# RWKV-7 chunk inverses on 64x64 tensor-engine tiles in place of 32x32 tiles, with other planner paces

## The chip, the core and the metric

The kernel runs on one core of one Trainium2 chip. The metric is device microseconds (us) of one execution. Engines are named as in the profile: PE (TensorE, matmul), PEld (its weight loads), DVE (VectorE), ACT (ScalarE), POOL (GpSimd), SP (SyncE, which only issues DMAs here).

## The reference

One layer of a hybrid decoder on 512 tokens of width 2048, float32: an input projection, then side by side an RG-LRU branch (4 heads of 256) and an RWKV-7 branch (16 heads of 64), an output projection, a gated FFN of width 6144 with a causal convolution, a gated per-layer embedding, and a final RMSNorm. The part that the change touches is the RWKV-7 scan. Cut to what matters:

```
def step(state, inp):                       # state: per head 64 x 64
    r_t, w_t, k_t, v_t, kk_t, b_t = inp     # b_t = kk_t * a_t
    sa = einsum('bhvk,bhk->bhv', state, -kk_t)
    state = state * w_t + outer(sa, b_t) + outer(v_t, k_t)
    y = einsum('bhvk,bhk->bhv', state, r_t)
```

A chunked form computes this for 64 tokens at once: within a chunk the terms `sa` depend on each other through a strictly triangular 64x64 matrix, so each chunk of each head needs the inverse of a unit triangular 64x64 matrix. There are 8 chunks and 16 heads, so 128 such inverses.

## The kernel before, in words

**Stages.** Phase 1 (about the first 870 us of the profile) holds the input projection, both branches and the half of the output projection that can be done so far. Phase 2 holds the rest of the output projection, the FFN and the gated embedding. Nearly all of the work is dense fp32 matmul done as three fp32r products (high x high, high x low, low x high; lines 156, 158, 160 in phase 1, and 1178 to 1180, 1260 to 1262, 1347 to 1349 in phase 2). Weights come by DMA on SP's queue (L114), ACT makes the high part (L121), DVE the low part (L127) or, for half of phase 1's tiles, POOL by an accumulating DMA (L125).

**The RWKV pairs.** Heads are handled in eight pairs j = 0 to 7; a pair fills the 128 partitions (head 0 in partitions 0 to 63, head 1 in 64 to 127). For each pair there are four generators. `prep(j)` makes the decays and the scaled operands. `batch(j)` makes, for all 8 chunks at once, the score matrices MQ and NQ (L732, L734), the inverse, and two products with it (L741). `chain(j)` carries the 64x64 state through the 8 chunks (L854 to L880). `norm(j)` normalises and gates the output (L889 to L904). `duo(j)` runs `chain(j-1)` and `batch(j)` in lockstep: in each step the chain's products are issued first and the batch's behind them.

**The inverse.** It is built by doubling. With blocks of b = 1, inverses of 2x2 blocks are written down directly from a mask (L765 to L768). For b = 2, 4, 8, 16 a level joins two b-blocks into one of 2b: a first group of products (L775, reads MQ and Tm), a masked copy into Gm by DVE (L785), a second group of products (L775, reads Tt and Gm), an addition into Tm by DVE (L803), and a transpose of Tm into Tt by DVE (L804). Before the change this runs on the four 32x32 diagonal blocks that a pair of heads has (two heads times two halves), so Tm and Tt are 128 x 256 and each group is 8 chunks x 4 blocks = 32 products with a 32-column stationary operand and 16 moving columns. In the trace each fp32 product is two MATMUL instructions, so a group shows as 64. The last join (32 to 64) is done apart: 16 products (L812), two ACT copies into Gm (L815), four ACT copies of Tt into the result TT (L817), 16 products (L825), and two ACT copies of the joined quarter into TT (L827). TT, 128 x 8 x 64, is cleared once at the start by POOL (L291). L741 then multiplies with TT.

**What sets the order.** PE's instruction order in phase 1 is written by a planner, `merge` (L352 to L416). It keeps a virtual time t in ns. A dense matmul costs 216. A step of a core generator (`duo`) yields a cost and a wait; its next step comes when t has passed the larger of that wait and a pace (L375: `dpace` = 3159 while pairs 1 to 7 run in lockstep, `pace` otherwise). `prep` and the two halves of `norm` ("tails") have waits of their own (`start`, `dec7`, `g2`, `g3`). In between, dense matmuls are issued. A dense matmul may also be held until a pair has been prepared or a pair's output is done: the last eight units of the output projection of phase 1 wait for the output of pair 6. The order on the other engines comes from a scheduler that goes by priority; `offw` is the priority of the weight pipeline (L100), `offs` of the core steps, `offd` of what follows dense matmuls, `offp` of prep's steps, `offt` of the transposed operands that `turn` makes (L747 to L753, four of them for each pair).

Of the kernel before, what the change touches and what calls it, by code (L numbers as in the profile page):

```python
# [6 lines left out]
AF = mybir.ActivationFunctionType  # L7
ALU = mybir.AluOpType
# [5 lines left out]
KT = D // 128  # L14
NB = 8

W = dict(offw=3000, offp=[0, 300, 0, 1000, 5000, -100, 466], offl=0, offt=0, pace=1007, dpace=3159, late=8560, offs=10000, offd=3000, start=1554, lora=5885, dec=0, rsk=12832, ready=23343, bonus=39298, t0=5900, tg=1601, tt=1464, lx=4233, lu=1319, ls=1435, g1=97321, g2=4936, g3=7972, per=[2, 3, 2, 2, 2, 2, 3, 0], dec7=6140)
DL = 1024
NP = 8
FF = 6144  # L20
# [2 lines left out]
C = 64  # L23
NC = S // C
# [12 lines left out]
for _n, _c in PCOLS:  # L37
# [1 line left out]
    _o += _c  # L39
PW = _o  # L40

CCOLS = [("ident", 128), ("ones1", 1), ("mask", 128)] + [("lev1", 32)] + [("lev%d" % b, 16) for b in (2, 4, 8, 16)] + \
        [("bd2", 2), ("id32", 32), ("odd", 2)]
CKEEP = 129
COFF = {}
_o = 0
# [6 lines left out]
def shape_constants():  # L53
    c = np.zeros((128, CW), np.float32)
    p = np.arange(128)
    s = p % 64
    t = np.arange(64)
    c[:, COFF["ident"]:COFF["ident"] + 128] = np.eye(128)
    o = COFF["mask"]
    c[:, o:o + 64] = s[:, None] < t[None, :]  # L60
    c[:, o + 64:o + 128] = s[:, None] <= t[None, :]

    r = (p % 32)[:, None]
    t = np.arange(32)[None, :]
    c[:, COFF["lev1"]:COFF["lev1"] + 32] = (t // 2 == r // 2) & (t % 2 == 1) & (r % 2 == 0)

    c[:, COFF["odd"]:COFF["odd"] + 2] = p[:, None] // 32 % 2 == np.arange(2)[None, :]

    for b in (2, 4, 8, 16):
        o = COFF["lev%d" % b]  # L70
        c[:, o:o + 16] = ((r // b) % 2 == 1) & (r // (2 * b) == t[:, :16] // b)
    o = COFF["id32"]
    c[:, o:o + 32] = r == t
    o = COFF["bd2"]
    c[:, o:o + 2] = p[:, None] // 64 == np.arange(2)[None, :]
    c[:, COFF["ones1"]] = 1.0
    return c


class Builder:  # L80
# [160 lines left out]
    def phase1(self):  # L241
# [3 lines left out]
        V, SC, G, TE = nc.vector, nc.scalar, nc.gpsimd, nc.tensor  # L245
# [42 lines left out]
        G.memset(self.scadd[:, :, 0:1], 1.0)  # L288

        self.TT = cp.tile([128, NC, C], F32, name="TT")  # L290
        G.memset(self.TT, 0.0)  # L291

        self.llo = cp.tile([128, 3, 128], F32R, name="llo")
        G.memset(self.llo.bitcast(F32), 0.0)
# [418 lines left out]
    def batch(self, j, q):  # L713
        nc, A, k1 = self.nc, self.A, self.k1
        V, SC, G, TE = nc.vector, nc.scalar, nc.gpsimd, nc.tensor
        T = lambda tag, bufs=1, shape=(128, S), dt=F32: self.t(k1, tag, shape, dt, bufs)
        wk = self.aux
        AR, bt, ktl, vt, pcs, bv, gt = q
        H2 = (slice(0, 64), slice(64, 128))
# [17 lines left out]
        def each(lhs, rhs, dst):  # L737
            ps = wk()
            for c in range(NC):
                for hs in H2:  # L740
                    TE.matmul(ps[hs, c * C:(c + 1) * C], lhs(hs, c), rhs(hs, c), start=True, stop=True)  # L741
            SC.activation(dst, c3(ps), AF.Copy)
# [14 lines left out]
            scores(bt, MQ, half)  # L757

        Q4 = [(slice(32 * g, 32 * g + 32), slice(32 * (g % 2), 32 * (g % 2) + 32)) for g in range(4)]
        Tm, Tt = T("Tm", 1, (128, 8, 32)), T("Tt", 1, (128, 8, 32))
        bc = lambda n, w: self.K(n).unsqueeze(1).broadcast_to([128, 8, w])
        for i, t_ in enumerate((Tm, Tt)):
            V.scalar_tensor_tensor(t_, MQ[:, :, 32 * i:32 * i + 32], self.K("odd")[:, i:i + 1], bc("lev1", 32), ALU.mult, ALU.mult)  # L765
        V.tensor_tensor(Tm, Tm, bc("id32", 32), ALU.add)
        V.tensor_tensor(Tt, Tt, Tm, ALU.add)
        V.transpose(fl(Tm), fl(Tt))  # L768
        yield 2160, W['t0']

        def prod(lhs, rhs):
            ps = wk()
            for i in range(8):
                for r_, c_ in Q4:
                    TE.matmul(ps[r_, i * 16:(i + 1) * 16], lhs(r_, c_, i), rhs(r_, i), start=True, stop=True)  # L775
            return ps[:, 0:128]
        TT = self.TT
        vk = ak = bk = kk2 = None
        for b in (2, 4, 8, 16):

            left = fl(Tm).rearrange("p (g h b) -> p g h b", h=2, b=b)[:, :, 0, :]
            ng = 16 // b
            ps = prod(lambda r_, c_, i: MQ[r_, i, c_], lambda r_, i: left[r_, i * ng:(i + 1) * ng, :])
            Gm = T("Gm", 1, (128, 8, 32))
            V.tensor_tensor(Gm[:, :, 0:16], ps.rearrange("p (i t) -> p i t", t=16), bc("lev%d" % b, 16), ALU.mult)  # L785
            if b == 2:
                scores(ktl, NQ, 0)
            with self.tc.high_priority(offset=W['offt'] - self.OFFS):
                if b == 2:

                    vk = turn("vk", vt, 2)
                    mv = T("mv", 1, (128, NC))
                    V.tensor_reduce(mv.unsqueeze(2), vk, mybir.AxisListType.X, ALU.add)
                    V.scalar_tensor_tensor(vk, mv.unsqueeze(2).broadcast_to([128, NC, C]), -1.0 / C, vk, ALU.mult, ALU.add)
                if b == 4:
                    ak = turn("ak", fl(AR[:, 0]), 1)
                if b == 8:
                    bk = turn("bk", bt, 2)
                if b == 16:
                    kk2 = turn("kk2", ktl, 2)  # L800
            yield 1100, W['tg']
            ps = prod(lambda r_, c_, i: Tt[r_, i, :], lambda r_, i: Gm[r_, i, 0:16])
            V.tensor_tensor(left, ps.rearrange("p (g b) -> p g b", b=b), left, ALU.add)  # L803
            V.transpose(fl(Tt), fl(Tm))  # L804
            if b == 2:
                scores(ktl, NQ, 1)
            yield 1100, W['tt']

        ps = wk()
        for i in range(8):  # L810
            for h in (0, 64):
                TE.matmul(ps[h + 32:h + 64, i * 32:(i + 1) * 32], MQ[h:h + 32, i, 32:64], Tm[h:h + 32, i, :], start=True, stop=True)  # L812
        Gm = T("Gm", 1, (128, 8, 32))
        for h in (32, 96):
            SC.activation(Gm[h:h + 32], ps[h:h + 32, 0:256].rearrange("p (i t) -> p i t", t=32), AF.Copy)  # L815
        for r_, c_ in Q4:
            SC.activation(TT[r_, :, c_], Tt[r_], AF.Copy)  # L817

        X1 = NQ[:, :, 0:64]
        each(lambda hs, c: NQ[hs, c, 0:64], lambda hs, c: vk[hs, c, :], X1)  # L820
        yield 1800, W['tg']
        ps = wk()
        for i in range(8):
            for h in (0, 64):
                TE.matmul(ps[h:h + 32, i * 32:(i + 1) * 32], Gm[h + 32:h + 64, i, :], Tt[h + 32:h + 64, i, :], start=True, stop=True)  # L825
        for h in (0, 64):
            SC.activation(TT[h:h + 32, :, 32:64], ps[h:h + 32, 0:256].rearrange("p (i t) -> p i t", t=32), AF.Copy)  # L827
        yield 860, W['tt']

        WT = MQ[:, :, 0:64]  # L830
        each(lambda hs, c: ak[hs, c, :], lambda hs, c: TT[hs, c, :], WT)
# [5 lines left out]
    def chain(self, j, q, u):  # L837
# [9 lines left out]
        for c in range(NC):  # L847
            yo = py[:, c * C:(c + 1) * C]
            us = NQ[:, c, 0:64]
            last = c == NC - 1  # L850
            if c:
                pu = ch()
                for hs in H2:
                    TE.matmul(pu[hs, 0:64], MQ[hs, c, 0:64], st[hs], start=True, stop=True)  # L854
                us = T("us", 2, (128, 64))
                V.tensor_tensor(us, pu[:, 0:64], NQ[:, c, 0:64], ALU.add)
            if not last:
                ps = ch()
                for hs in H2:
                    TE.matmul(ps[hs, 0:64], kk2[hs, c, :], vk[hs, c, :], start=True, stop=False)  # L860
            for hs in H2:
                TE.matmul(yo[hs], vk[hs, c, :], NQ[hs, c, 64:128], start=True, stop=False)
            if c:
                for hs in H2:
                    TE.matmul(yo[hs], st[hs], AR[hs, 1, c, :], start=False, stop=False)
                yield 700, W['lu']
            if not last:
                for hs in H2:
                    TE.matmul(ps[hs, 0:64], bk[hs, c, :], us[hs], start=False, stop=True)
                pc = pcs[:, c:c + 1]  # L870
                sn = T("st", 2, (128, 64))
                if c == 0:
                    V.tensor_scalar(sn, ps[:, 0:64], pc, None, ALU.mult)
                else:
                    so = T("so", 2, (128, 64))
                    SC.activation(so, st, AF.Copy, scale=pc)
                    V.scalar_tensor_tensor(sn, ps[:, 0:64], pc, so, ALU.mult, ALU.add)
                st = sn
            for hs in H2:
                TE.matmul(yo[hs], us[hs], MQ[hs, c, 64:128], start=False, stop=True)  # L880
            yield 500, W['ls']
# [628 lines left out]
```

## Time and profile before

| what | value |
|---|---|
| median of 3 runs | 2689.41 us (2687.48 to 2691.31) |
| the profiled execution's own time | 2688.0 us |
| its span, first to last instruction | 2686.2 us |
| mean granted TensorE clock | 0.992 |
| PE busy | 2636.5 us, 98% of the span |
| DVE, ACT, POOL busy | 1684.7, 1096.7, 328.5 us |

The span is the profiled execution's time less 1.8 us that lie around it. PE is busy nearly everywhere, so the time is read from PE: from what its instructions take, from where it waits, and from the clock that it is granted. A row of the timeline is: start in us from the span's start, length in us, engine, line and operation, output tile and input tiles, shape of the stationary operand and of the moving one, and the number of instructions merged in the row. Lengths overlap, since matmuls are pipelined; what a group costs PE is the distance from its start to the start of the next row.

### The profile page before, as it was taken

How to read it: one execution, taken by the hardware profiler on the slowest of the kernel's cores; microseconds unless marked ns; L12 is line 12 of the kernel's file. 1: busy time of each engine (PE TensorE's matmuls, PEld its weight loads, DVE VectorE, ACT ScalarE, POOL GpSimd, SP SyncE). 2: the span in 40 equal slices, each digit the busy share in tenths (PEclk: the TensorE clock that was granted, in tenths of full speed). 3: DMA queues.
4: the chain of work that ended last, by engine and by line, in shares of the span. 5: the costliest groups of instructions: out<-in, count | busy, mean ns of one | idle time of the engine just before them, and what ended most of it. 6: DMA issues, size and time to landing. Idle time of an engine off the chain costs nothing.

```text
span 2686.2 us, 43499 instructions
## 1 busy us (share of the span) xinstructions
PE 2636.5 (98%) x18440; PEld 2170.1 (81%) x18440; DVE 1684.7 (63%) x2268; ACT 1096.7 (41%) x1532; POOL 328.5 (12%) x266
## 2 busy tenths in 40 slices
PE   8999999999999999999999999999999999999996
PEld 7887787877777888888888888888888888888886
DVE  6664865667554734667666766766666667775235
ACT  6563555547433533333333333333333333334344
POOL 4120211211131310000000000000000000000013
PEclk9999999999999999999999999999999999999998
DMA  6544443444462422322322223222232222232222
GB/s 191 144 101 102 107 110 92 109 114 105 131 171 67 146 86 88 109 101 96 110 102 94 103 94 110 94 102 102 96 108 102 102 102 102 95 113 87 94 88 101
DMA packets 89235, 286.99 MB, mean 107 GB/s; under 512 B 10320, under 2 KB 13008, under 8 KB 89040
## 3 DMA queue, kind: packets, MB, share of 16 engines
q1 hardware_dynamic: 81984, 258.52, 28.4%
q0 software_dynamic: 7056, 25.69, 5.7%
q8 instruction: 144, 2.36, 0.4%
q14 instruction: 51, 0.42, 0.0%
HBM read 276.05 MB, written 8.13 MB: 106 GB/s over the span
## 4 chain that ended last, share of the span: by engine, by line
PE 91%; DVE 4%; DMA 2%; ACT 1%; POOL 1%; issue 1%; SPq 0%; DVEq 0%; POOLq 0%; ACTq 0%
PE wk L1178 12%; PE wk L1180 12%; PE wk L1179 12%; PE mm L160 7%; PE mm L158 7%; PE mm L156 7%; PE mm L1262 6%; PE mm L1260 6%; PE mm L1261 6%; PE mm L1348 2%; PE mm L1349 2%; PE mm L1347 2%; PE wk L775 2%; PE mm L1178 1%; PE mm L1180 1%; PE mm L1179 1%
## 5 line engine op out<-in xcount | busy, mean ns | idle before, releaser
L121 ACT ACTIVATE whi<-wraw 128x1024 fp32r<-128x1024 f32 (+2 forms) x363 | 375.4, 1034 | 738.5 <-PE mm L158 193.1
L1178 PE MATMUL wk<-uh,whi 128*128 128x512 f32 x1408 | 547.8, 389 | 0.0
L1179 PE MATMUL wk<-ul,whi 128*128 128x512 f32 x1408 | 547.7, 389 | 0.0
L1180 PE MATMUL wk<-uh,wlo 128*128 128x512 f32 x1408 | 547.7, 389 | 0.0
L127 DVE TENSOR_TENSOR wlo<-wraw,whi 128x1024 fp32r<-128x1024 f32 (+2 forms) x314 | 380.6, 1212 | 213.4 <-ACT whi L121 208.5
L121 ACT ACTIVATE whi<-hw 128x1024 fp32r<-128x1024 f32 x154 | 163.2, 1060 | 464.3 <-PE wk L1179 418.6
L160 PE MATMUL mm<-xh,wlo 128*128 128x512 f32 x832 | 333.5, 401 | 7.1 <-DMA wlo<-wz 7.1
L156 PE MATMUL mm<-xh,whi 128*128 128x512 f32 x832 | 331.2, 398 | 1.6 <-DVE y L895 1.6
L158 PE MATMUL mm<-xl,whi 128*128 128x512 f32 x832 | 330.5, 397 | 0.0
L1180 PEld LDWEIGHTS wk<-uh,wlo 128*128 128x128 f32 x1408 | 264.3, 188 | 54.9
L1179 PEld LDWEIGHTS wk<-ul,whi 128*128 128x128 f32 x1408 | 264.3, 188 | 54.8
L1178 PEld LDWEIGHTS wk<-uh,whi 128*128 128x128 f32 x1408 | 264.3, 188 | 54.8
L127 DVE TENSOR_TENSOR wlo<-hw,whi 128x1024 fp32r<-128x1024 f32 x154 | 188.6, 1225 | 181.2 <-ACT whi L121 178.8
L1261 PE MATMUL mm<-wlo,hid 128*128 128x512 f32 x680 | 265.1, 390 | 0.0
L1262 PE MATMUL mm<-whi,hid 128*128 128x512 f32 x680 | 264.8, 389 | 0.0
L1260 PE MATMUL mm<-whi,hid 128*128 128x512 f32 x680 | 264.8, 389 | 0.0
L1206 POOL TENSOR_TENSOR tmp<-tmp,rsa 128x512 f32<-128x512 f32 x48 | 87.4, 1822 | 1360.9 <-ACT tmp L1205 1360.9
L160 PEld LDWEIGHTS mm<-xh,wlo 128*128 128x128 f32 x832 | 156.9, 189 | 42.2 <-DMA wlo<-wz 8.0
L156 PEld LDWEIGHTS mm<-xh,whi 128*128 128x128 f32 x832 | 157.1, 189 | 35.8 <-issue 4.5
L158 PEld LDWEIGHTS mm<-xl,whi 128*128 128x128 f32 x832 | 157.0, 189 | 34.1 <-issue 2.0
L1275 DVE TENSOR_TENSOR h<-h,mm 128x512 f32<-128x512 f32 x264 | 174.8, 680 | 0.7
L1261 PEld LDWEIGHTS mm<-wlo,hid 128*128 128x128 f32 x680 | 127.6, 188 | 26.4
(475 smaller groups left out, 3744.0 us busy)
## 6 DMA issues: line engine op xcount, KB each, us to landing
wraw<-wgu SPq DMA_DIRECT2D x192, 512.0 KB, 3.2
hw<-wd SPq DMA_DIRECT2D x88, 512.0 KB, 3.2
wraw<-wz SPq DMA_DIRECT2D x80, 512.0 KB, 3.6
wlo<-wz POOLq DMA_DIRECT2D x40, 512.0 KB, 5.6
wraw<-wpg SPq DMA_DIRECT2D x31, 512.0 KB, 3.2
wraw<-wo SPq DMA_DIRECT2D x22, 512.0 KB, 3.3
wraw<-wo SPq DMA_DIRECT2D x20, 256.0 KB, 2.9
tmp<-xT SPq DMA_DIRECT2D x16, 256.0 KB, 2.8
```

The source lines that it names most:

```text
L121: nc.scalar.activation(hi, raw, AF.Copy)
L127: nc.vector.tensor_tensor(lo, raw, hi.bitcast(F32), ALU.subtract)
L156: nc.tensor.matmul(ps, hi[:, k, :], xh, start=first and i == 0, stop=False)
L158: nc.tensor.matmul(ps, hi[:, k, :], xl, start=False, stop=False)
L160: nc.tensor.matmul(ps, lo[:, k, :], xh, start=False, stop=last and i == n - 1)
L1178: TE.matmul(ps, wh[:, k, :], xh, start=h + k == 0, stop=False)
L1179: TE.matmul(ps, wh[:, k, :], xl, start=False, stop=False)
L1180: TE.matmul(ps, wl[:, k, :], xh, start=False, stop=h == 1 and k == 7)
L1260: TE.matmul(ps, x[0][:, k, ts_], w[0][:, k, :], start=first and k == 0, stop=False)
L1261: TE.matmul(ps, x[0][:, k, ts_], w[1][:, k, :], start=False, stop=False)
L1262: TE.matmul(ps, x[1][:, k, ts_], w[0][:, k, :], start=False, stop=last and k == 1)
L1275: V.tensor_tensor(o, o, ps[tt], op)
```

## The change

The level loop runs on whole 64x64 chunk matrices: Tm and TT are 128 x 8 x 64 and block diagonal, and the loop has a fifth level, b = 32, in place of the last join done apart. Each group of products is 8 chunks x 2 heads = 16 products with a 64-column stationary operand (MQ or TT) and 32 moving columns. Gm becomes 128 x 256, the transpose of each level 128 x 512. The fifth level's Gm is made by one ACT copy with a 0/1 scale per partition, and its result, the joined quarter, is transposed straight from PSUM into TT by two DVE transposes. The ACT copies at L815, L817 and L827 and POOL's clearing of TT go. Constants are wider (64 and 32 columns in place of 32 and 16). The chain's tiles `us` and `so` have one buffer in place of two. Planner costs and paces change in one line: weight pipeline priority 3000 to 20000, `offd` 3000 to 1000, `offt` 0 to 1000, second entry of `offp` 300 to -100, `pace` 1007 to 1625, `start` 1554 to 1071, `t0` 5900 to 6100, `tg` 1601 to 1750, `tt` 1464 to 2431, `lu` 1319 to 1861, `ls` 1435 to 1231, `g3` 7972 to 13054, `dec7` 6140 to 5046; `dpace`, `late` and the rest stay, and `lx` and `g1` are read nowhere in the code.

```diff
--- before.py
+++ after.py
@@ -14,7 +14,7 @@
 KT = D // 128
 NB = 8
 
-W = dict(offw=3000, offp=[0, 300, 0, 1000, 5000, -100, 466], offl=0, offt=0, pace=1007, dpace=3159, late=8560, offs=10000, offd=3000, start=1554, lora=5885, dec=0, rsk=12832, ready=23343, bonus=39298, t0=5900, tg=1601, tt=1464, lx=4233, lu=1319, ls=1435, g1=97321, g2=4936, g3=7972, per=[2, 3, 2, 2, 2, 2, 3, 0], dec7=6140)
+W = dict(offw=20000, offp=[0, -100, 0, 1000, 5000, -100, 466], offl=0, offt=1000, pace=1625, dpace=3159, late=8560, offs=10000, offd=1000, start=1071, lora=5885, dec=0, rsk=12832, ready=23343, bonus=39298, t0=6100, tg=1750, tt=2431, lx=25915, lu=1861, ls=1231, g1=259468, g2=4936, g3=13054, per=[2, 3, 2, 2, 2, 2, 3, 0], dec7=5046)
 DL = 1024
 NP = 8
 FF = 6144
@@ -39,8 +39,8 @@
     _o += _c
 PW = _o
 
-CCOLS = [("ident", 128), ("ones1", 1), ("mask", 128)] + [("lev1", 32)] + [("lev%d" % b, 16) for b in (2, 4, 8, 16)] + \
-        [("bd2", 2), ("id32", 32), ("odd", 2)]
+CCOLS = [("ident", 128), ("ones1", 1), ("mask", 128)] + [("lev1", 64)] + [("lev%d" % b, 32) for b in (2, 4, 8, 16)] + \
+        [("bd2", 2), ("id64", 64), ("half", 1)]
 CKEEP = 129
 COFF = {}
 _o = 0
@@ -60,17 +60,17 @@
     c[:, o:o + 64] = s[:, None] < t[None, :]
     c[:, o + 64:o + 128] = s[:, None] <= t[None, :]
 
-    r = (p % 32)[:, None]
-    t = np.arange(32)[None, :]
-    c[:, COFF["lev1"]:COFF["lev1"] + 32] = (t // 2 == r // 2) & (t % 2 == 1) & (r % 2 == 0)
-
-    c[:, COFF["odd"]:COFF["odd"] + 2] = p[:, None] // 32 % 2 == np.arange(2)[None, :]
+    r = s[:, None]
+    t = t[None, :]
+    o = COFF["lev1"]
+    c[:, o:o + 64] = (t // 2 == r // 2) & (t % 2 == 1) & (r % 2 == 0)
 
     for b in (2, 4, 8, 16):
         o = COFF["lev%d" % b]
-        c[:, o:o + 16] = ((r // b) % 2 == 1) & (r // (2 * b) == t[:, :16] // b)
-    o = COFF["id32"]
-    c[:, o:o + 32] = r == t
+        c[:, o:o + 32] = ((r // b) % 2 == 1) & (r // (2 * b) == t[:, :32] // b)
+    c[:, COFF["half"]] = s >= 32
+    o = COFF["id64"]
+    c[:, o:o + 64] = r == t
     o = COFF["bd2"]
     c[:, o:o + 2] = p[:, None] // 64 == np.arange(2)[None, :]
     c[:, COFF["ones1"]] = 1.0
@@ -288,7 +288,6 @@
         G.memset(self.scadd[:, :, 0:1], 1.0)
 
         self.TT = cp.tile([128, NC, C], F32, name="TT")
-        G.memset(self.TT, 0.0)
 
         self.llo = cp.tile([128, 3, 128], F32R, name="llo")
         G.memset(self.llo.bitcast(F32), 0.0)
@@ -757,32 +756,30 @@
             scores(bt, MQ, half)
 
 
-
-        Q4 = [(slice(32 * g, 32 * g + 32), slice(32 * (g % 2), 32 * (g % 2) + 32)) for g in range(4)]
-        Tm, Tt = T("Tm", 1, (128, 8, 32)), T("Tt", 1, (128, 8, 32))
-        bc = lambda n, w: self.K(n).unsqueeze(1).broadcast_to([128, 8, w])
-        for i, t_ in enumerate((Tm, Tt)):
-            V.scalar_tensor_tensor(t_, MQ[:, :, 32 * i:32 * i + 32], self.K("odd")[:, i:i + 1], bc("lev1", 32), ALU.mult, ALU.mult)
-        V.tensor_tensor(Tm, Tm, bc("id32", 32), ALU.add)
-        V.tensor_tensor(Tt, Tt, Tm, ALU.add)
-        V.transpose(fl(Tm), fl(Tt))
-        yield 2160, W['t0']
+        Tm, TT = T("Tm", 1, (128, NC, C)), self.TT
+        bc = lambda n, w: self.K(n).unsqueeze(1).broadcast_to([128, NC, w])
+        V.tensor_tensor(TT, MQ[:, :, 0:64], bc("lev1", 64), ALU.mult)
+        V.tensor_tensor(TT, TT, bc("id64", 64), ALU.add)
+        V.transpose(fl(Tm), fl(TT))
+        yield 1900, W['t0']
 
         def prod(lhs, rhs):
             ps = wk()
-            for i in range(8):
-                for r_, c_ in Q4:
-                    TE.matmul(ps[r_, i * 16:(i + 1) * 16], lhs(r_, c_, i), rhs(r_, i), start=True, stop=True)
-            return ps[:, 0:128]
-        TT = self.TT
+            for i in range(NC):
+                for hs in H2:
+                    TE.matmul(ps[hs, i * 32:(i + 1) * 32], lhs[hs, i, 0:64], rhs(hs, i), start=True, stop=True)
+            return ps[:, 0:256]
         vk = ak = bk = kk2 = None
-        for b in (2, 4, 8, 16):
+        for b in (2, 4, 8, 16, 32):
 
             left = fl(Tm).rearrange("p (g h b) -> p g h b", h=2, b=b)[:, :, 0, :]
-            ng = 16 // b
-            ps = prod(lambda r_, c_, i: MQ[r_, i, c_], lambda r_, i: left[r_, i * ng:(i + 1) * ng, :])
-            Gm = T("Gm", 1, (128, 8, 32))
-            V.tensor_tensor(Gm[:, :, 0:16], ps.rearrange("p (i t) -> p i t", t=16), bc("lev%d" % b, 16), ALU.mult)
+            ng = 32 // b
+            ps = prod(MQ, lambda hs, i: left[hs, i * ng:(i + 1) * ng, :])
+            Gm = T("Gm", 1, (128, NC, 32))
+            if b < 32:
+                V.tensor_tensor(Gm, ps.rearrange("p (i t) -> p i t", t=32), bc("lev%d" % b, 32), ALU.mult)
+            else:
+                SC.activation(fl(Gm), ps, AF.Copy, scale=self.K("half"))
             if b == 2:
                 scores(ktl, NQ, 0)
             with self.tc.high_priority(offset=W['offt'] - self.OFFS):
@@ -798,34 +795,21 @@
                     bk = turn("bk", bt, 2)
                 if b == 16:
                     kk2 = turn("kk2", ktl, 2)
-            yield 1100, W['tg']
-            ps = prod(lambda r_, c_, i: Tt[r_, i, :], lambda r_, i: Gm[r_, i, 0:16])
-            V.tensor_tensor(left, ps.rearrange("p (g b) -> p g b", b=b), left, ALU.add)
-            V.transpose(fl(Tt), fl(Tm))
+            if b == 32:
+
+                X1 = NQ[:, :, 0:64]
+                each(lambda hs, c: NQ[hs, c, 0:64], lambda hs, c: vk[hs, c, :], X1)
+            yield (900 if b < 32 else 1800), W['tg']
+            ps = prod(TT, lambda hs, i: Gm[hs, i, :])
+            if b < 32:
+                V.tensor_tensor(left, ps.rearrange("p (g b) -> p g b", b=b), left, ALU.add)
+                V.transpose(fl(TT), fl(Tm))
+            else:
+                for h in (0, 64):
+                    V.transpose(TT[h:h + 32, :, 32:64], ps[h + 32:h + 64].rearrange("p (i t) -> p i t", t=32))
             if b == 2:
                 scores(ktl, NQ, 1)
-            yield 1100, W['tt']
-
-        ps = wk()
-        for i in range(8):
-            for h in (0, 64):
-                TE.matmul(ps[h + 32:h + 64, i * 32:(i + 1) * 32], MQ[h:h + 32, i, 32:64], Tm[h:h + 32, i, :], start=True, stop=True)
-        Gm = T("Gm", 1, (128, 8, 32))
-        for h in (32, 96):
-            SC.activation(Gm[h:h + 32], ps[h:h + 32, 0:256].rearrange("p (i t) -> p i t", t=32), AF.Copy)
-        for r_, c_ in Q4:
-            SC.activation(TT[r_, :, c_], Tt[r_], AF.Copy)
-
-        X1 = NQ[:, :, 0:64]
-        each(lambda hs, c: NQ[hs, c, 0:64], lambda hs, c: vk[hs, c, :], X1)
-        yield 1800, W['tg']
-        ps = wk()
-        for i in range(8):
-            for h in (0, 64):
-                TE.matmul(ps[h:h + 32, i * 32:(i + 1) * 32], Gm[h + 32:h + 64, i, :], Tt[h + 32:h + 64, i, :], start=True, stop=True)
-        for h in (0, 64):
-            SC.activation(TT[h:h + 32, :, 32:64], ps[h:h + 32, 0:256].rearrange("p (i t) -> p i t", t=32), AF.Copy)
-        yield 860, W['tt']
+            yield 900, W['tt']
 
         WT = MQ[:, :, 0:64]
         each(lambda hs, c: ak[hs, c, :], lambda hs, c: TT[hs, c, :], WT)
@@ -852,7 +836,7 @@
                 pu = ch()
                 for hs in H2:
                     TE.matmul(pu[hs, 0:64], MQ[hs, c, 0:64], st[hs], start=True, stop=True)
-                us = T("us", 2, (128, 64))
+                us = T("us", 1, (128, 64))
                 V.tensor_tensor(us, pu[:, 0:64], NQ[:, c, 0:64], ALU.add)
             if not last:
                 ps = ch()
@@ -872,7 +856,7 @@
                 if c == 0:
                     V.tensor_scalar(sn, ps[:, 0:64], pc, None, ALU.mult)
                 else:
-                    so = T("so", 2, (128, 64))
+                    so = T("so", 1, (128, 64))
                     SC.activation(so, st, AF.Copy, scale=pc)
                     V.scalar_tensor_tensor(sn, ps[:, 0:64], pc, so, ALU.mult, ALU.add)
                 st = sn
```

## The prediction

> **What bounds the kernel now.** I read the page first, then the windows of phase 1, then PE's waits, and last PE's timeline around the inverse.
>
> ```profile
> span 2686.2 us, 43499 instructions
> PE 2636.5 (98%) x18440; PEld 2170.1 (81%) x18440; DVE 1684.7 (63%) x2268; ACT 1096.7 (41%) x1532; POOL 328.5 (12%) x266
> ```
>
> ```profile
> 203.00:205.90 2.90, 0.38 (x14) 0.24 (x9) 2.87 (x6) 0.36 (x1) 0.00 (x0) 1.00 0.16 30
> 205.90:212.80 6.90, 5.25 (x86) 4.40 (x87) 5.38 (x11) 3.45 (x4) 0.86 (x1) 0.51 0.59 163
> 831.40:843.80 12.40, 8.82 (x134) 7.37 (x133) 5.47 (x15) 3.81 (x9) 3.30 (x2) 0.74 0.14 42
> 60.00:870.00 810.00, 795.29 (x10008) 636.67 (x10007) 493.43 (x850) 418.56 (x663) 142.81 (x127) 0.99 0.44 113
> ```
>
> The columns are window, length, busy time of PE, PEld, DVE, ACT and POOL, granted clock, DMA share, GB/s. In the 810 us of phase 1 that hold the inverses PE is idle for 14.7 us; DVE is busy for 493 and ACT for 419. So phase 1 is bound by PE, whose order is fixed by the planner: what a product takes on PE goes into the time one for one, and what DVE and ACT take does not, unless PE waits for it. It seldom does:
>
> ```profile
> PE mm L160 <- DMA wlo<-wz: 7.1, 2, 3.8
> PE wk L775 <- DVE Tm L768: 4.9, 2, 4.2
> PE wk L775 <- DVE Gm L785: 0.7, 1, 0.7
> ```
>
> Columns: total us, times, longest. Of 64 groups of L775, three waited for DVE. The 4.2 us one, at 203.4, is followed by the window with granted clock 0.51: 5.25 us of PE work at half speed, another 2.6 us. That stall is worth 6.8 us; the second DMA wait (7.1 - 3.8) 3.3 us. Phase 2 isn't touched.
>
> **The change part by part: products.** PE's timeline, before:
>
> ```profile
> 142.24 0.73 PE L775 MATMUL wk<-Tm,MQ 32*32 32x16 f32 x64
> 142.89 0.50 PE L156 MATMUL mm<-xh,whi 128*128 128x512 f32 x1
> ...
> 154.92 0.95 PE L912 MATMUL wk<-con,tmp 128*128 128x2 f32 x8
> 155.80 0.73 PE L775 MATMUL wk<-Gm,Tt 32*32 32x16 f32 x64
> ...
> 158.27 0.69 PE L812 MATMUL wk<-Tm,MQ 32*32 32x32 f32 x32
> 158.89 1.15 PE L741 MATMUL wk<-vk,NQ 64*64 64x64 f32 x32
> 159.97 0.50 PE L156 MATMUL mm<-xh,whi 128*128 128x512 f32 x1
> ```
>
> ```profile
> 240.13 0.28 PE L865 MATMUL y<-AR,st 64*64 64x64 f32 x4
> 240.34 0.73 PE L775 MATMUL wk<-Tm,MQ 32*32 32x16 f32 x64
> 241.00 0.50 PE L158 MATMUL mm<-xl,whi 128*128 128x512 f32 x1
> ...
> 255.41 0.28 PE L880 MATMUL y<-MQ,us 64*64 64x64 f32 x4
> 255.62 0.69 PE L825 MATMUL wk<-Tt,Gm 32*32 32x32 f32 x32
> 256.24 0.50 PE L158 MATMUL mm<-xl,whi 128*128 128x512 f32 x1
> ```
>
> ```profile
> 260.27 0.28 PE L865 MATMUL y<-AR,st 64*64 64x64 f32 x4
> 260.38 1.10 PE L741 MATMUL wk<-TT,ak 64*64 64x64 f32 x32
> 261.32 1.10 PE L741 MATMUL wk<-NQ,TT 64*64 64x64 f32 x32
> 262.35 0.50 PE L634 MATMUL wk<-wx,lhi 128*128 128x512 f32 x1
> ```
>
> No row has a 64x64 tile with 32 moving columns, so its cost must be bounded. A group of L775 is 64 instructions on four tiles, 16 on each, with 16 moving columns: 0.66 us from start to next start. A group of L825 is 32 instructions on two tiles, again 16 on each, with twice the moving columns: 0.62. Neither the number of instructions nor the columns that move set the time; the 16 loads of a 32-column stationary operand on each tile do. L912 shows the load alone: two moving columns, 128 stationary ones, 0.88/8 = 0.11 us each. With 64 stationary columns L741 takes 0.94 us for 16 loads on each of two tiles (260.38 to 261.32), 0.059 us a load. Per load that is 0.039 (0.62/16, with the change of tile shape in it), 0.059 and 0.11 us for 32, 64 and 128 columns: it grows with the stationary width. The new group makes 16 loads of 64 columns on each of two tiles, so I take L741's price, 0.94; the other end, if the 32 moving columns set it, is L825's 0.62. The page "TensorE: Matmul & The Clock Gate" of the Trainium skill (section "LDWEIGHTS (loading the stationary operand)") says that a load takes the stationary columns over 1.2 GHz, whatever the rows: an estimate by it is 53 ns for 64 columns, 0.85 us a group, and the sum below would be some 7 us less than by the row (0.09 less for each of 80 groups); it speaks against the change all the same.
>
> Changing the tile shape costs something too. From L865's start to the next group it is 0.11 us where that keeps 64x64 (260.27), 0.21 where it goes to 32x32 (240.13). In pairs 1 to 7 every group stands behind the chain's 64x64 products, so the change saves 0.10 at the entry. L741 in front of dense work takes 1.03 (261.32), behind a 32x32 group 1.08 (158.89), so a 64x64 group that follows gains 0.05.
>
> - Pairs 1 to 7, levels 4, 8, 16, both groups, chain in front and dense behind: 1.03 - 0.66 - 0.10 = +0.27, 42 times: 11.3 us.
> - The last join's second group: 1.03 - 0.62 - 0.10 = +0.31, 7 times: 2.2.
> - Level 2, score products behind: 0.94 - 0.66 - 0.10 - 0.05 = +0.13, 14 times: 1.8.
> - The last join's first group, L741 behind: 0.94 - 0.62 - 0.10 - 0.05 = +0.17, 7 times: 1.2.
> - Pair 0 has no chain in front. Its groups between dense work go from 0.65 (142.24) to 1.08, 0.43 six times; the last join's second +0.46; its first and level 2's two, with a 64x64 group behind, take 0.94 + 0.05 at the entry - 0.05 behind, so +0.32 and 2 x +0.28: 3.9 together.
>
> Sum +20.4 us. With L825's price for the group (0.32 less for each of 80) it would be 25.6 less, -5.2.
>
> **DVE and ACT.**
>
> ```profile
> L753 DVE STREAM_TRANSPOSE kk<-kk 128x512 f32<-128x512 f32 x8 | 5.6, 704 | 10.0 <-ACT kk L752 10.0
> L734 DVE TENSOR_TENSOR MQ<-wk,con 128x512 f32<-128x512 f32 x16 | 10.6, 680 | 4.3 <-PE wk L732 4.3
> L804 DVE STREAM_TRANSPOSE Tt<-Tm 128x256 f32<-128x256 f32 x32 | 14.1, 440 | 0.9
> L803 DVE TENSOR_TENSOR Tm<-wk,Tm 128x128 f32<-128x128 f32 x32 | 9.1, 286 | 11.2 <-PE wk L775 11.2
> L785 DVE TENSOR_TENSOR Gm<-wk,con 128x128 f32<-128x128 f32 x32 | 9.1, 285 | 14.8 <-PE wk L775 14.7
> L765 DVE SCALAR_TENSOR_TENSOR Tt<-MQ,con 128x256 f32<-128x256 f32 x8 | 5.9, 739 | 0.0
> L767 DVE TENSOR_TENSOR Tt<-Tt,Tm 128x256 f32<-128x256 f32 x8 | 4.1, 518 | 0.1
> L765 DVE SCALAR_TENSOR_TENSOR Tm<-MQ,con 128x256 f32<-128x256 f32 x8 | 3.8, 471 | 0.2
> L768 DVE STREAM_TRANSPOSE Tm<-Tt 128x256 f32<-128x256 f32 x8 | 3.5, 438 | 0.1
> L766 DVE TENSOR_TENSOR Tm<-Tm,con 128x256 f32<-128x256 f32 x8 | 3.3, 416 | 0.0
> ```
>
> ```profile
> L817 ACT ACTIVATE TT<-Tt 32x256 f32<-32x256 f32 x32 | 13.2, 414 | 3.7 <-DVE Tt L804 3.4
> L815 ACT ACTIVATE Gm<-wk 32x256 f32<-32x256 f32 x16 | 6.0, 375 | 7.3 <-PE wk L812 6.9
> L827 ACT ACTIVATE TT<-wk 32x256 f32<-32x256 f32 x16 | 5.9, 370 | 3.8 <-PE wk L825 3.6
> ```
>
> Per pair, the start of the inverse goes from 0.74 + 0.47 + 0.42 + 0.52 + 0.44 = 2.6 us of DVE to a product, an addition and a transpose of 512 columns, 0.68 + 0.68 + 0.70 = 2.1. A level goes from 0.29 + 0.29 + 0.44 to 0.42 + 0.42 + 0.70, +0.5, four times. The two transposes of the quarter, priced as L804's 256 columns, add 0.9. DVE: -0.5 + 2.1 + 0.9 = +2.5 us a pair, 20 in all, in 810 us of which 317 are free. ACT loses 4 x 0.41 + 4 x 0.37 and gains one copy of 0.38: -2.7 a pair. Both I cost at nothing: what hides them is the dense work between two steps, `dpace` 3159/216 = 15 matmuls, so 3.4 us at the 0.23 us that the rows show for one, against at most 0.27 (chain) + 0.42 + 0.70 of DVE. If that cover fails, each of the 14 groups in a pair could lose the 0.5. The quarter's transposes wait for PE on DVE's queue, where the low parts of weights and the chain's next state stand behind them; before, it was ACT that waited. The next core step is a pace later, so I price it at 0 to 0.3 us a pair, and take 0.
>
> **Paces and priorities.** `dpace` is kept and is over `tg` and `tt`, so the lockstep keeps its 15 matmuls; `t0` gives 29 instead of 28 in front of a pair's first group. Pair 0, alone, gets longer waits, filled by dense work. So the first wait for Tm has 0.5 less to wait for on DVE and 0.2 more in front: -0.7. At the end of phase 1 dense work is held until pair 6 is normalised (the window at 831.4). By the planner's sums `g3` + `pace` put one more step of the last chain ahead of that; ten steps lie in those 12.4 us, 1.2 each, less 0.4 for PE's own work: +0.9 (0 to 2). Priorities: the two large stalls (6.8 and 3.3 us) come from the order on ACT, DVE and POOL, which the new numbers rewrite. Between none gone (0) and both gone (-10.1), I take -2.5, near none, since the waits of 0.7 show that any order makes stalls of its own.
>
> Sum: 20.4 - 0.7 + 0.9 - 2.5 = +18.1 us. The profiled execution took 2688.0 (span 2686.2 and 1.8 around it), so 2706.1 for one like it; it stood 1.4 under the median, so the median goes to 2707.5, rounded 2708.
>
> **Rivals.** A difference under 0.2% (5.4 us) is about what a measurement of this kernel can't tell from none.
>
> 1. *The stalls go.* Priority 20000 for weights and earlier transposed operands clear both large stalls and the two waits of 0.7: 20.4 + 0.9 - 10.1 - 1.4 = +9.8, so 2699. For it: the 4.2 us wait and the DMA wait are matters of order on ACT. Against: PE's 14.7 us of idle time bound it.
> 2. *Faster: the instruction count sets a group's time.* Halving 64 instructions to 32 then brings a group from 0.66 to 0.33, and the 64 groups of L775 give back 64 x 0.33 = 21 us; the saved entries add 70 x 0.10 = 7, and the 16 groups of the last join stay. Even half of it is -14: 2675. It decides if a 64x64 group with 32 columns takes under 0.68 us, where the sum above is zero. Against: L825 has half of L775's instructions and takes the same. "TensorEngine Tiling (Array Packing)" of the Trainium skill (section "Performance Considerations") has this rule: some 60 cycles for each matmul however few columns, so that fewer and wider ones win. By that rule the trace should show L825 at half of L775; it shows 0.62 against 0.66, and doesn't agree.
> 3. *More stalls.* Weight copies of about 1.2 us pushed ahead of the core's operations on DVE make PE wait in a pair's levels: 2 us a pair, +16: 2724. It needs delays over the some 2 us of slack (3.4 less 1.4). Against: three waits in 64 groups now.
> 4. *No change:* the longer groups fall where PE would have waited. That needs 20 of 14.7 us, so it works only together with stalls that go: 2689.
>
> **How the numbers follow.** Forecast 0.57 (its own range 2700 to 2718: 20.4 - 0.7 + 0.9 = 20.6 without the item for stalls, less 10.1 if both go, or 6.8 and 1.1 more if one like that at 203.4 comes on top and the end takes its 2); rival 1 0.17, of which 0.05 lies within 0.2%; rival 2 0.10; rival 3 0.11; rival 4 0.05. So faster 0.10, same 0.10, slower 0.80. The range 2692 to 2722 leaves out rivals 2 and 4 and half of rival 3, 0.20.
>
> **What would show it.** A new product group should stand in PE's timeline as x32 with 64*64 and 64x32, 0.94 us to a 64x64 group and 1.03 to a dense row; under 0.7 refutes the sum. The rows for L804's and L785's successors should be 0.70 and 0.42 us, and PE's waits for them should stay under a few us. PE's busy time should grow by about 20 us, phase 2's windows should be unchanged. A window with granted clock 0.5 in the middle of phase 1 tells whether a stall like that at 203.4 is there again.

## The result, and the profile after

| kernel | median us | runs |
|---|---|---|
| before | 2691.98 (2687.48 to 2692.92) | 6 |
| after | 2712.59 (2709.71 to 2714.6) | 6 |

The ratio is 1.0079, with a 95% interval of 1.0066 to 1.0092: slower by 18 to 25 us. (The three further runs of the kernel before lie at 2692.7 to 2692.9, so its median is now 2.6 above the one that the prediction started from.) The profiled execution of the kernel after took 2714.6 us, the slowest of its six.

The page of the kernel after, its first two lines:

```profile
span 2712.8 us, 39388 instructions
PE 2660.9 (98%) x16392; PEld 2199.4 (81%) x16392; DVE 1700.2 (63%) x2268; ACT 1074.5 (40%) x1475; POOL 330.8 (12%) x265
```

PE has 2048 MATMULs fewer and is busy for 24 us more. Phase 1 is counted here up to the first product of L1178 (L1162 in the kernel after), at 939.1 us before and 966.1 after; "about the first 870 us" above leaves out the last dense products of L156 to L160. Windows of the kernel after: phase 1 as a whole, each stretch with a granted clock near 0.5 in it, the same 810 us as in the prediction, and phase 2.

```profile
0.00:966.10 966.10, 938.47 (x8545) 765.13 (x8545) 598.70 (x967) 467.61 (x717) 197.44 (x179) 0.98 0.44 117
38.70:45.50 6.80, 5.89 (x19) 4.83 (x20) 2.84 (x7) 4.93 (x11) 4.75 (x4) 0.50 0.65 183
318.60:322.00 3.40, 3.40 (x19) 2.68 (x16) 2.23 (x6) 0.00 (x0) 1.65 (x3) 0.50 0.47 154
448.30:451.70 3.40, 3.40 (x9) 2.65 (x8) 3.22 (x6) 0.35 (x1) 1.21 (x1) 0.50 0.83 145
475.60:482.40 6.80, 6.35 (x24) 4.70 (x25) 4.03 (x8) 6.20 (x13) 1.34 (x2) 0.50 0.21 77
694.00:697.40 3.40, 3.40 (x21) 2.78 (x17) 2.87 (x5) 0.46 (x1) 3.16 (x3) 0.51 0.58 116
864.70:871.50 6.80, 5.37 (x78) 4.86 (x78) 2.03 (x8) 0.80 (x3) 1.67 (x1) 0.50 0.00 0
...
60.00:870.00 810.00, 792.27 (x7782) 644.14 (x7782) 496.78 (x826) 387.95 (x592) 142.92 (x126) 0.99 0.43 110
...
966.10:2712.80 1746.70, 1722.39 (x7849) 1434.28 (x7847) 1101.46 (x1301) 606.86 (x759) 133.31 (x86) 0.99 0.32 99
```

The same windows of the kernel before, phase 1, the two half-clock stretches not yet shown, and phase 2:

```profile
0.00:939.10 939.10, 914.01 (x10592) 735.86 (x10593) 583.67 (x967) 489.97 (x773) 195.03 (x180) 0.99 0.45 121
38.70:45.50 6.80, 5.07 (x16) 4.07 (x17) 3.04 (x8) 4.77 (x11) 4.63 (x4) 0.50 0.66 182
837.40:844.20 6.80, 5.62 (x71) 4.85 (x71) 2.34 (x8) 1.32 (x3) 1.66 (x1) 0.50 0.01 2
...
939.10:2686.20 1747.10, 1722.49 (x7849) 1434.25 (x7847) 1101.04 (x1301) 606.69 (x759) 133.45 (x86) 0.99 0.29 99
```

Phase 2 is the same to 0.4 us, so all of it is in phase 1, which is 27.0 us longer in the profiled executions. These split in three. **Work:** PE's busy time, less half of what lies in stretches at half clock, is 914.0 - (5.1 + 5.3 + 5.6)/2 = 906.0 before and 938.5 - (5.9 + 3.4 + 3.4 + 6.4 + 3.4 + 5.4)/2 = 924.6 after: +18.5. **Idle:** 939.1 - 914.0 = 25.1 against 27.6: +2.5. **Clock:** 8.0 lost before, 13.9 after: +5.9. The two profiled executions are not typical: that of before lies 4.0 under its median, that of after 2.0 over. By the medians the kernel lost 20.6 us, so that beside 18.5 of work some 2 us are left for idle time and clock together.

PE's timeline of the kernel after, around three groups of pair 1, the first with score products behind it:

```profile
215.75 1.07 PE L770 MATMUL wk<-Gm,TT 64*64 64x32 f32 x32
216.66 1.07 PE L731 MATMUL wk<-AR,ktl 64*64 64x128 f32 x16
...
231.57 0.28 PE L849 MATMUL y<-AR,st 64*64 64x64 f32 x4
231.69 1.07 PE L770 MATMUL wk<-Tm,MQ 64*64 64x32 f32 x32
232.69 0.50 PE L156 MATMUL mm<-xh,whi 128*128 128x512 f32 x1
...
236.48 0.28 PE L864 MATMUL y<-MQ,us 64*64 64x64 f32 x4
236.60 1.07 PE L770 MATMUL wk<-Gm,TT 64*64 64x32 f32 x32
237.60 0.50 PE L156 MATMUL mm<-xh,whi 128*128 128x512 f32 x1
```

A group takes 1.00 us to the dense row behind it and 0.91 to another 64x64 group, from start to start, and stands 0.12 behind the start of the chain's last products instead of 0.21. PE's waits after, by total; three of before are in the prediction:

```profile
PE wk L770 <- DVE Tm L763: 5.3, 3, 2.2
PE mm L160 <- DMA wlo<-wz: 3.3, 1, 3.3
...
PE mm L156 <- ACT lt L963: 2.8, 1, 2.8
PE wk L915 <- DVE Gm L780: 2.1, 1, 2.1
```

The 4.2 us wait for Tm has become one of 2.2, the one of 0.7 has gone, and two of 1.5 and 1.7 have come elsewhere; the second DMA wait (3.3) has gone, and waits for ACT (2.8) and for Gm (2.1) have come. DVE and ACT, the rows that answer to those of before:

```profile
L806 DVE STREAM_TRANSPOSE TT<-Tm 128x512 f32<-128x512 f32 x32 | 22.6, 707 | 0.7
L805 DVE TENSOR_TENSOR Tm<-wk,Tm 128x256 f32<-128x256 f32 x32 | 13.5, 421 | 17.2 <-PE wk L770 16.8
L780 DVE TENSOR_TENSOR Gm<-wk,con 128x256 f32<-128x256 f32 x32 | 13.5, 421 | 23.5 <-PE wk L770 23.5
L809 DVE STREAM_TRANSPOSE TT<-wk 32x256 f32<-32x256 f32 x16 | 7.2, 448 | 1.6 <-PE wk L770 1.2
```

```profile
L782 ACT ACTIVATE Gm<-wk,con 128x256 f32<-128x256 f32 x8 | 3.7, 468 | 10.2 <-PE wk L770 10.2
```

### The profile page after: what moved, and what is told of

Same layout as the page of the kernel before. It is cut to its first block, busy times and chain, and to the rows that moved or that the text cites. A ratio compares the mean times of both kernels' runs of the same rounds, so it can differ in the third digit from the quotient of the medians.

```text
span 2712.8 us, 39388 instructions
## 1 busy us (share of the span) xinstructions
PE 2660.9 (98%) x16392; PEld 2199.4 (81%) x16392; DVE 1700.2 (63%) x2268; ACT 1074.5 (40%) x1475; POOL 330.8 (12%) x265
## 4 chain that ended last, share of the span: by engine, by line
PE 90%; DVE 4%; ACT 3%; issue 1%; POOL 1%; DMA 1%; SPq 0%; DVEq 0%; POOLq 0%; ACTq 0%
PE wk L1164 12%; PE wk L1162 12%; PE wk L1163 12%; PE mm L160 7%; PE mm L156 7%; PE mm L158 7%; PE mm L1246 6%; PE mm L1244 6%; PE mm L1245 6%; PE wk L770 3%; PE mm L1331 2%; PE mm L1333 2%; PE mm L1332 2%; PE mm L1162 1%; PE mm L1164 1%
## 5 line engine op out<-in xcount | busy, mean ns | idle before, releaser
L1162 PE MATMUL wk<-uh,whi 128*128 128x512 f32 x1408 | 547.8, 389 | 0.0
L127 DVE TENSOR_TENSOR wlo<-wraw,whi 128x1024 fp32r<-128x1024 f32 (+2 forms) x314 | 378.0, 1204 | 221.5 <-ACT whi L121 216.6
L156 PE MATMUL mm<-xh,whi 128*128 128x512 f32 x832 | 333.6, 401 | 5.8 <-ACT lt L963 2.8
L160 PE MATMUL mm<-xh,wlo 128*128 128x512 f32 x832 | 333.4, 401 | 3.3 <-DMA wlo<-wz 3.3
L1162 PEld LDWEIGHTS wk<-uh,whi 128*128 128x128 f32 x1408 | 264.3, 188 | 54.8
L127 DVE TENSOR_TENSOR wlo<-hw,whi 128x1024 fp32r<-128x1024 f32 x154 | 188.7, 1225 | 181.2 <-ACT whi L121 178.7
L156 PEld LDWEIGHTS mm<-xh,whi 128*128 128x128 f32 x832 | 158.2, 190 | 41.0 <-ACT lt L963 3.2
L160 PEld LDWEIGHTS mm<-xh,wlo 128*128 128x128 f32 x832 | 157.9, 190 | 39.2 <-DMA wlo<-wz 3.7
L1246 PEld LDWEIGHTS mm<-whi,hid 128*128 128x128 f32 x680 | 127.7, 188 | 26.4
```

The source lines that it names most:

```text
L127: nc.vector.tensor_tensor(lo, raw, hi.bitcast(F32), ALU.subtract)
L156: nc.tensor.matmul(ps, hi[:, k, :], xh, start=first and i == 0, stop=False)
L160: nc.tensor.matmul(ps, lo[:, k, :], xh, start=False, stop=last and i == n - 1)
L1162: TE.matmul(ps, wh[:, k, :], xh, start=h + k == 0, stop=False)
L1246: TE.matmul(ps, x[1][:, k, ts_], w[0][:, k, :], start=False, stop=last and k == 1)
```

## The experiments

**Theory L:** a group costs its loads, 16 of 64 stationary columns on each tile, and this extra work on PE is the bulk of the loss. **Rivals:** C, the moving columns (or a fixed cost for a group) set the price; P, the new paces made the loss through stalls and clock. Later came Q, that the weight pipeline's priority makes the largest stalls, against T, that the steps' paces do. All ratios are to runs of the kernel before on the same chip, whose median was 2689.9 in the first four experiments, 2689.6 in the next four, 2689.9 in 9 to 11 and 2690.1 in 12; the result above was taken against 2692.0, so two experiments are compared by their ratios.

**1. The changed kernel with the old planner line** (`W = dict(offw=3000, ...)` of the kernel before).

> The changed kernel with the planner line of the kernel before. Theory L (a group of products costs 16 loads of its 64 stationary columns on each tile, and that is the bulk of the loss): the products still cost 18 us more than before, by the changed kernel's rows (1.00 us to dense work in place of 0.66, less 0.10 at the entry, and so on, 80 groups), so about 2692 + 18 = 2710 us, give or take 6 for stalls of its own. Rival P (the new paces made the loss, through stalls and low clock): the time goes back to 2692 to 2697.

Measured: 2741.05 us, ratio 1.0188 (1.0175 to 1.0202). Both expectations failed. PE's waits and the chain around the longest of them:

```profile
PE mm L160 <- DMA wlo<-wz: 32.1, 5, 14.7
PE wk L770 <- DVE Tm L763: 3.5, 2, 1.8
```

```profile
298.44 3.31 DVE lrc L603 x4
...
301.89 1.28 POOL lt L974
...
303.40 0.64 POOL lt L977
304.04 0.64 issue
304.68 6.35 DMA wlo<-wz
311.03 0.04 issue
311.07 0.79 PE mm L160
```

POOL's accumulating DMA, which finishes the low part of a weight tile, is issued only behind RG-LRU work on POOL that waits for DVE's reciprocals (L603); PE stands still from 296.4 to 311.1, and the transfer itself is 6.35 us of that. The new paces didn't make the loss; the old ones make it worse on this kernel.

**2. The kernel before with the new planner line.**

> The kernel before with the planner line of the changed kernel. Theory L: the 32x32 groups keep their 0.66 us, so the time stays at 2692 us, plus up to 8 if the new paces make more waits for PE as they did in the changed kernel (3 us more idle time of PE and some 6 us lost to low clock there). Rival P: 2708 to 2712.

Measured: 2694.16 us, ratio 1.0017 (1.0008 to 1.0025), +4.3 us. P is refuted; L's upper part holds: the new line costs some us through stalls and clock.

**3. Twice as many products of half the columns.** The group's code, cut; the two calls pass half k of the moving columns.

```diff
             for i in range(NC):
-                for hs in H2:
-                    TE.matmul(ps[hs, i * 32:(i + 1) * 32], lhs[hs, i, 0:64], rhs(hs, i), start=True, stop=True)
+                for k in range(2):
+                    for hs in H2:
+                        TE.matmul(ps[hs, i * 32 + 16 * k:i * 32 + 16 * k + 16], lhs[hs, i, 0:64], rhs(hs, i, k), start=True, stop=True)
```

> The changed kernel, each product of 32 moving columns issued as two of 16 with the same stationary operand: 32 loads on each tile instead of 16, the same columns in all. Theory L: a group goes from 0.91 to about 32 x 0.058 = 1.86 us, 80 groups, +75 us: about 2787 us. Rival C (the columns that move set a group's time, or a fixed cost for each group): a group stays under 1.1 us and the time within 10 us of 2712.6.

Measured: 2785.38 us, ratio 1.036 (1.0344 to 1.0376). Its timeline:

```profile
268.14 1.99 PE L771 MATMUL wk<-Tm,MQ 64*64 64x16 f32 x64
269.98 1.13 PE L740 MATMUL wk<-vk,NQ 64*64 64x64 f32 x32
```

32 loads on each tile take 1.84 us, 0.058 each, with 16 moving columns; the kernel before had 0.059 with 64. C is refuted: the same columns moved, and the group took twice as long.

**4. 64x32 tiles: the same products split by stationary columns.**

```diff
             for i in range(NC):
-                for hs in H2:
-                    TE.matmul(ps[hs, i * 32:(i + 1) * 32], lhs[hs, i, 0:64], rhs(hs, i), start=True, stop=True)
+                for q in range(2):
+                    for h in (0, 64):
+                        TE.matmul(ps[h + 32 * q:h + 32 * q + 32, i * 32:(i + 1) * 32], lhs[h:h + 64, i, 32 * q:32 * q + 32],
+                                  rhs(slice(h, h + 64), i), start=True, stop=True)
```

> The changed kernel, each product split by its stationary columns: 64 rows by 32 columns, four tiles, 16 loads of 32 columns on each, 32 columns moving. Theory L with loads that are independent on each tile: 16 x 0.032 = 0.51 us, so a group drops from 0.91 to about 0.55, 80 x 0.36 = 29 us less, with 0.10 more at an entry that changes the tile shape (70 times, 7 us): about 2691 us. If loads into the same 64 rows go one after the other: 32 x 0.032 = 1.0 us a group and 0.1 for the entry, about 2728 us. Rival C: 2713 to 2720, the same columns moving.

Measured: 2695.25 us, ratio 1.0022 (1.0014 to 1.0031): 15 us off the changed kernel by the ratios (1.0079 there).

```profile
226.84 0.28 PE L851 MATMUL y<-AR,st 64*64 64x64 f32 x4
227.06 0.76 PE L771 MATMUL wk<-Tm,MQ 64*32 64x32 f32 x64
227.74 0.50 PE L156 MATMUL mm<-xh,whi 128*128 128x512 f32 x1
```

The same operands and the same moving columns, and 0.68 in place of 1.00, with 64 instructions in place of 32; the entry takes 0.22 in place of 0.12, as the tile shape changes. The loads are half as wide and lie on four tiles instead of two, 16 on each as before. Two tiles on the same 64 rows load side by side: one after the other was expected to take 1.0 us and 0.1 for the entry.

**5 to 8. Where the waits come from.** The edits are single numbers of the planner line: 5 is experiment 1 with `offw=20000`; 6 is the changed kernel with `offw=3000`; 7 is the kernel before with `offw=20000`; 8 is the kernel before with `t0=7000`.

> The changed kernel with the planner line of the kernel before, but the weight pipeline's priority kept at 20000. The run with the whole old line took 2741, with 32 us of PE's waits on the accumulating weight DMA. Theory Q (the low priority of the weight pipeline makes those waits: its ACT, DVE and POOL steps queue behind the core's and the RG-LRU's): they shrink to under 8 us and the time goes to 2710 to 2716. Rival T (the steps' paces make them: t0, tg, tt, g3 and the rest): the time stays over 2730.

Measured: 2707.25 us, ratio 1.0066 (1.0052 to 1.008). The waits for the weight DMA shrink to 5.4 us. As Q had it; the time is a little under the range. Against the new line (1.0079) it is 3 us by the ratios, and the two intervals overlap.

> The changed kernel with the weight pipeline's priority alone put back to 3000. Theory Q: PE's waits on the weight DMA grow to 15 to 30 us and the time goes to 2728 to 2741. Rival T: it stays within 5 us of 2712.6.

Measured: 2715.57 us, ratio 1.0098 (1.0084 to 1.0112), 5.3 us of waits on the weight DMA. As T had it: the low priority alone doesn't make the long waits, so Q alone isn't enough.

> The kernel before with the weight pipeline's priority alone raised to 20000. If Q is a property of the pipeline and not of the new products: the two waits for the weight DMA (7.1 us) shrink to about one (3.8), others may come where the core's DVE steps stand behind weights; 2690 give or take 4. If the products decide which priority is good: it gets slower, 2695 to 2705.

Measured: 2693.22 us, ratio 1.0015 (1.0007 to 1.0024). The DMA waits fall from 7.1 to 4.7 us, and the waits for Tm rise from 4.9 to 9.6: the first expectation, with other waits in place of those that went.

> The kernel before with t0 at 7000 in place of 5900: 32 dense matmuls in place of 27 to 28 in front of a pair's first group, so 1.1 us more for DVE and ACT. If the 4.2 us wait at 203 and the low clock behind it come from too little distance: the wait falls to 3.1 us or less, the low clock goes, 2 to 4 us less, 2686 to 2688. If any change of the order makes stalls elsewhere: within 5 us of 2690, with waits at other places.

Measured: 2694.41 us, ratio 1.0017 (1.0008 to 1.0026). At the place itself (207.6) the wait falls to 1.9, behind a new one of 1.0 for the weight DMA, and the low clock goes, as the first expectation had it. But the time doesn't fall: there are two more waits for Tm (one of 3.3) and three in all for the weight DMA (8.0 us). That is the second expectation.

**9. 64x32 tiles with the planner line of experiment 5.**

> Products split into 64x32 tiles as in the run of that name, with the planner line of the kernel before and the weight pipeline's priority at 20000. Theory L, the parts adding up: 64x32 tiles took 17 us off the changed kernel, this planner line 5 us, so 2690 us, level with the kernel before (2690); its groups take 0.69 us to the next start against 0.66 and 0.62 before, 80 groups, 3 us more, so it shouldn't beat it by more than 2. Rival T (stalls follow the order and not the products): anywhere from 2688 to 2700.

Measured: 2708.68 us, ratio 1.0073 (1.0059 to 1.0087). The sum of parts fails by 19 us. The products cost what they do in 4 (work 910 in the table below); the stalls don't add up, as rival T had it, though the time lies over T's range too. Its waits:

```profile
PE wk L771 <- DVE Tm L763: 7.2, 1, 7.2
PE mm L958 <- ACT lxh L139: 4.8, 1, 4.8
PE mm L160 <- DMA wlo<-wz: 4.1, 1, 4.1
PE wk L917 <- DVE tmp L910: 3.7, 1, 3.7
```

**10. Each level's transpose on DVE twice** (the line `V.transpose(fl(TT), fl(Tm))` of the level loop repeated).

> The changed kernel with each level's transpose on DVE issued twice: 0.7 us more of DVE behind 32 of the levels' additions, 22.6 us of DVE in all, which nothing but the next product group waits for. If DVE is covered by the dense work between steps, as costed at nothing: within 6 us of 2712.6. If DVE's longer levels are on the path: 2725 to 2735.

Measured: 2712.1 us, ratio 1.0082 (1.0068 to 1.0096), against 1.0079 without. The two transposes in its rows:

```profile
L806 DVE STREAM_TRANSPOSE TT<-Tm 128x512 f32<-128x512 f32 x32 | 22.7, 708 | 0.7
L807 DVE STREAM_TRANSPOSE TT<-Tm 128x512 f32<-128x512 f32 x32 | 22.4, 699 | 0.5
```

22.4 us more of DVE, right in front of the product groups, cost nothing that can be measured: the first expectation.

**11 and 12.** 11 is experiment 1 with `offd=1000`; 12 is the changed kernel with all four old priorities (`offw=3000`, `offd=3000`, `offt=0`, second `offp` 300) and its own paces.

> The changed kernel with the planner line of the kernel before, but the priority of what follows dense matmuls at 1000 in place of 3000. The whole old line gave 2741 and 32 us of waits on the weight DMA; priority 20000 for the weights alone took them away. If priorities are what makes these waits, and the weights and the RG-LRU work sink together with this number: they stay, over 2730. If the RG-LRU work alone sinks, the weights come first and the time goes to 2707 to 2716.

Measured: 2736.37 us, ratio 1.0168 (1.0155 to 1.0182), 29.2 us of waits on the weight DMA: they stay, the first expectation.

> The changed kernel with all four priorities of the kernel before (weights 3000, after dense work 3000, transposed operands 0, prep 300), its own paces kept. The whole old line gave 2741 and 32 us of waits on the weight DMA; the weights' priority alone put back gave 2715.6, and of the old line with priority 20000 2707. If the old priorities together make these waits: over 2730 again, with 25 us or more of them. If the old paces are needed for them: 2710 to 2718.

Measured: 2717.78 us, ratio 1.0103 (1.0086 to 1.0119), 6.6 us of them: the second expectation. So on the changed kernel the long DMA waits need two things together, the low priority of the weight pipeline (5 removes them) and the old paces (12 and 6 haven't got them). The kernel before has both and waits 7.1 us, so they need the new body too. Which of the paces wasn't tried, nor what in the body.

**All runs in one account.** For each profiled execution: where phase 2 begins, PE's work at full clock up to there (worked out as above), and the rest, which is idle time plus what half clock cost.

| products | planner line | phase 2 begins | work | rest |
|---|---|---|---|---|
| 32x32 | old (before) | 939 | 906 | 33 |
| 32x32 | new (2) | 947 | 906 | 41 |
| 32x32 | old, offw 20000 (7) | 943 | 907 | 36 |
| 32x32 | old, t0 7000 (8) | 945 | 906 | 39 |
| 64x64 | new (after) | 966 | 925 | 41 |
| 64x64 | old (1) | 991 | 926 | 65 |
| 64x64 | old, offw 20000 (5) | 961 | 927 | 34 |
| 64x64 | new, offw 3000 (6) | 969 | 925 | 43 |
| 64x64 | old, offd 1000 (11) | 983 | 926 | 57 |
| 64x64 | new paces, old priorities (12) | 972 | 926 | 47 |
| 64x64, transposes twice | new (10) | 964 | 926 | 38 |
| 64x32 | new (4) | 944 | 910 | 34 |
| 64x32 | old, offw 20000 (9) | 958 | 910 | 49 |
| 64x64, twice the loads | new (3) | 1036 | 999 | 37 |

The work goes with the products, within 2 us, whatever the planner line; the rest goes with the order and ranges from 33 to 65 us. The single buffers of `us` and `so` weren't tried apart: they are in every run of the changed kernel. None of the runs beats the kernel before.

## Why the prediction was right

The direction, the range and the mechanism of the loss held: 2708 was forecast, 2712.6 measured. The size is closer than its parts deserve, and that is luck: of +18.1 forecast and +20.6 measured, the products were some 2 us too high, and the three other terms together (-2.3) some 4 too low, by the medians. Of the gap from 2707.5 to 2712.6, another 2.6 us is the median of before, which rose.

- **Products, +20.4.** Shown, and 1 to 2 us too large. Work rose by 18.5 us between the two profiles, and by 19 to 20 over the rows of the table. The price of a group was taken from L741's 0.94 and 1.03; it is 0.91 and 1.00, so the largest item (42 groups) is 1.00 - 0.66 - 0.10 = +0.24 rather than +0.27, and the whole list comes to about 18. That the loads on one tile and their stationary width set it, which the prediction could only bound, is shown by experiments 3 and 4 together.
- **Entry, -0.10.** Shown: 0.12 in place of 0.21.
- **Rival 2, the instruction count.** Refuted: 32 instructions take 0.91 to 1.00 us, 64 take 0.68 on 64x32 tiles and 1.84 on 64x64 tiles. The rule that the prediction weighed, of "TensorEngine Tiling (Array Packing)" in the Trainium skill, section "Performance Considerations", of some 60 cycles for each matmul however few its columns, does not order these three; the load time of "TensorE: Matmul & The Clock Gate" in the Trainium skill, section "LDWEIGHTS (loading the stationary operand)", does, with 0.058 us measured for 64 columns where it gives 53 ns.
- **DVE and ACT at nothing.** Right. The new rows (0.71, 0.42, 0.45 us) are as priced, but for the copy on ACT (0.47 instead of 0.38); DVE's whole busy time rose by 15.5 us and not by 20, since other rows came out shorter (L127's, 380.6 to 378.0, among them). PE has no wait for the quarter's transposes (L809) in its list. Experiment 10 puts another 22.4 us of DVE time on top and moves nothing.
- **First wait, -0.7.** Right in sign, too small: the wait at 203.4 went from 4.2 to 2.2 us, and the low clock behind it is gone. How much of that came from the shorter start on DVE and how much from `t0` isn't shown: in 2, old body and new line, the wait is 3.3; in 1, new body and old line, it is 1.8, but there a wait of 1.2 for the weight DMA stands 6 us ahead of it.
- **End of phase 1, +0.9.** From the first held step to the first dense row, 858.3 to 871.5 less the one dense product in between, against 831.5 to 843.8: about +0.6.
- **Stalls, -2.5.** This is the term that failed. Idle time and clock together, with the first wait and the end in them, rose by 8.4 us in the profiled executions and by some 2 by the medians, where -2.3 was forecast: new waits of 1.3 to 2.8 us came, and four stretches of low clock lie in the middle of phase 1 in place of one. Experiment 2 gives the planner line's price on the old products by medians, +4.3 (2 to 7). The products' 19 and this 4 make 23, within the measured 18 to 25.

Rival 3 had the right sign for the rest, but not its place: no level lost time regularly (the waits are single ones). Rivals 1 and 4 did not come.

## What to carry to other kernels

Price small fp32 products on tiles of PE (16 to 64 moving columns here) by loads on one tile times the time of a load, which grows with the stationary width, and not by instructions or by moving columns. Where the same work can be cut into narrower stationary operands on more tiles, it gets cheaper although the count doubles: 0.68 us in place of 1.00 in experiment 4. In a kernel that PE bounds, keep two accounts: PE's work at full clock, which adds up from rows to a microsecond or two, and idle time plus low clock, which belongs to the whole order and doesn't add up. A planner line has no worth apart from the body: going from the new line back to the old one gained 4 us on the old products and cost 29 us on the new ones.

## What the runs showed of the hardware that was not expected

Low clock needs no long gap. Windows of the kernel after, a stretch at half clock with the 3.4 us ahead of it:

```profile
444.90:448.30 3.40, 3.04 (x52) 2.72 (x51) 2.80 (x7) 3.40 (x7) 1.82 (x2) 1.00 0.56 164
448.30:451.70 3.40, 3.40 (x9) 2.65 (x8) 3.22 (x6) 0.35 (x1) 1.21 (x1) 0.50 0.83 145
```

PE was idle for 0.36 us of the 3.4 ahead, and the rest was mostly small products. The stretch costs half its length, 1.7 us. Idle time isn't needed at all: in experiment 3, PE was busy throughout the 3.4 us ahead of a stretch at half clock, mostly with small products.

```profile
583.20:586.60 3.40, 3.40 (x80) 3.28 (x79) 0.51 (x3) 1.65 (x3) 1.67 (x1) 1.00 0.00 0
586.60:590.00 3.40, 3.40 (x17) 2.75 (x14) 2.49 (x6) 1.39 (x2) 0.00 (x0) 0.50 0.00 0
```

Nor is idle time enough: behind the first wait of the kernel after, with PE busy for 1.53 us of 3.4, the clock stayed at 1.00.

```profile
206.20:209.60 3.40, 1.53 (x21) 1.00 (x19) 3.40 (x6) 0.36 (x1) 0.00 (x0) 1.00 0.36 140
209.60:213.00 3.40, 3.11 (x53) 2.77 (x54) 2.18 (x5) 2.28 (x3) 0.68 (x1) 1.00 0.30 83
```

What about the small products lowers the clock was not tried.
